# A two-layer streaming encoder: each feed-forward in two phases, and both parts of x in one 512 wide matmul

## The chip, the core and the metric

The kernel runs on one core of a Trainium2 chip. A time is the device time of one execution in microseconds (us), and less is better. TensorE multiplies a 128x128 block of weights that it holds with a stream of columns and adds the result into one of eight PSUM banks of 512 float32 columns. VectorE and ScalarE read PSUM and the on-chip memory and write back to the latter; GpSimd adds squares here. Every engine runs its own queue of instructions in order and waits for the others by semaphores.

## The reference

Two layers work on 256 tokens of width 1024. Each layer is, with all norms, gates and mixers cut to their names:

```
h = h + 0.5 * swiglu(rmsnorm(h, ffn1_norm), ffn1_w_up, ffn1_w_down)
h = h + token_mixer(rmsnorm(h, mix_norm), ...) @ w_out      # attention, retention, SSD, HGRN2
h = h + 0.5 * swiglu(rmsnorm(h, ffn2_norm), ffn2_w_up, ffn2_w_down)
gate = sigmoid(rmsnorm(h, ple_norm) @ ple_w_gate)
h = h + gate * (p[i] @ ple_w_proj)

def swiglu(h, w_up, w_down):
    gate, up = split(h @ w_up, 2)                           # 1024 -> 2 x 2816
    return (silu(gate) * up) @ w_down                       # 2816 -> 1024
```

A final rmsnorm ends it. All data are float32. The four feed-forwards (two in each layer) hold most of the arithmetic.

## The kernel before

The state `H` lies transposed: features on the 128 partitions, in eight tiles (`KD`) of 256 tokens (`S`) each. A product in nearly float32 precision is made of rounded operands: every weight and every x is split into a high part of the type float32r and the low rest, and three matmuls add high x high, high weight x low x, and low weight x high x. Line 247 in `prod` issues these three, each 256 columns wide.

Weights come as tiles of 128x1024 in the order of their use. `fetch` (line 155) loads one from memory on SyncE's queue into one of four `raw` buffers, ScalarE casts it to `wh` (line 164), VectorE subtracts to get `wl` (line 165), each with eight buffers. `weight` keeps two tiles fetched ahead in the program's order; a scheduler then orders each engine's queue, so that casts move forward until buffers are wanting.

A norm's scale is applied late: `Norm.part` (line 187) only multiplies by the norm's weight and splits (ScalarE line 192, VectorE line 193), `square` (line 200) squares on ScalarE and adds up on GpSimd, `scale` and `spread` sum the squares with small matmuls (line 108) and make a row `rb` of 1/rms for all tokens. It multiplies the results of the up matmuls, not x.

`ffn` (line 296) goes through 11 blocks `j` of 256 hidden columns. For each it makes gate and up (32 triples of matmuls into one bank of the kind `p` and one of the kind `m`), and then the part of the down product for the block before (16 triples into four banks of the kind `a`, which collect all 1024 output features over all j). Beside that VectorE and ScalarE make the product silu(gate) x up, 512 wide, and split it (lines 317 to 320 and `split`). After the last block `advance` (line 896) takes the four pairs of output tiles one after the other: `ffn_finish` scales and adds to `H`, `part` prepares the next x. The next stage's first group of matmuls runs over k in the outer loop, so that it can begin with the first pair.

After the second feed-forward of a layer the input p is loaded on ScalarE's queue (line 1016) and split. In layer 1 it is multiplied by `ple_w_proj` into four banks before the gate; in layer 2 `ending` does the same with tokens on the partitions, 512 columns wide (lines 924 to 926, gate in lines 937 to 939).

Of the kernel before, what the change touches and what calls it, by code (L numbers as in the profile page):

```python
# [9 lines left out]
F32 = mybir.dt.float32  # L10
# [9 lines left out]
P = 128  # L20
# [44 lines left out]
def trunk(ctx, tc, x, pt, par_d, con_d, w_d, ws_d, fin_d, out):  # L65
# [10 lines left out]
    cnt = [0]  # L76
    NB = {"h2": 4, "hp2": 1, "s2": 2, "m2": 7, "yh": 8, "yl": 8, "raw": 4, "wh": 8, "wl": 8}
    PB = {"p": 2, "m": 2, "a": 4}

    def T(shape, kind, dt=F32, bufs=2):  # L80
        cnt[0] += 1
        return wk.tile(shape, dt, name=f"{kind}_{cnt[0]}", tag=kind, bufs=bufs)

    def tw(kind, dt=F32, width=1024):
        if kind in ("raw", "wh", "wl"):
            return T([P, WIDE], kind, dt, NB[kind])[:, 0:width]
        return T([P, 512], kind, dt, NB[kind])

    def bank(which):
# [4 lines left out]
    def v2(t):  # L94
        return t.rearrange("p (a b) -> p a b", a=2)
# [33 lines left out]
    for t in kts + qts:  # L129
        G.memset(t, 0.0)  # L130
    xbp = cp.tile([P, 4, S + 3], F32, name="xbp")
    G.memset(xbp[:, :, 0:3], 0.0)
    identb = cp.tile([P, P], BF16, name="identb")
# [49 lines left out]
    class Norm:  # L183
        def __init__(self):
            self.h, self.l, self.sq = [], [], []

        def part(self, c, l, name, first=False):
            xh, xl = v2(tw("yh", F32R)), v2(tw("yl", F32R))
            for i in range(2):
                d = 2 * c + i  # L190
                w = prm(l, name, d)
                A.mul(xh[:, i], H[:, d], w)  # L192
                V.scalar_tensor_tensor(xl[:, i], H[:, d], w, xh[:, i].bitcast(F32),  # L193
                                       ALU.mult, ALU.subtract)
                self.h.append(xh[:, i])
                self.l.append(xl[:, i])
            if not first:
                self.square(c)

# [22 lines left out]
        def spread(self):  # L222
            for t in range(2):
                rows(self.b[:, 256 + t * P:256 + (t + 1) * P], self.col[:, t:t + 1])
            rb = cp.tile([P, S], F32, name=f"rb{cnt[0]}", tag="rb")
            A.copy(rb, self.b[:, 256:512])
            self.rb = rb.unsqueeze(1).broadcast_to([P, 2, S])

# [20 lines left out]

    def col_tiles(targets, xn, k_outer=False, arrival=None, lag=0):  # L250
        def one(b, w, m, k, terms=(0, 1, 2)):
            wh, wl = w[m]
            prod(b[:, m * S:(m + 1) * S], wh[:, k], wl[:, k], xn.h[k], xn.l[k],
                 k == 0 and m == 0, k == KD - 1, terms)
        if k_outer:
            units = [(b, w, m) for b, w in targets for m in range(2)]
            rank = arrival or (lambda u, k: k // 2)
            order = sorted((rank(u, k), u, k) for u in range(len(units)) for k in range(KD))
            for n in range(len(order) + lag):
                if n == len(order) * SCALE_AT // 32:  # L260
                    xn.scale()
                if n < len(order):
                    one(*units[order[n][1]], order[n][2], (0, 1))
                if n >= lag:
                    one(*units[order[n - lag][1]], order[n - lag][2], (2,))
            xn.spread()
        else:
            for b, w in targets:
                for m in range(2):
                    for k in range(KD):  # L270
                        one(b, w, m, k)

# [17 lines left out]
    def split(src):  # L290
        yh, yl = tw("yh", F32R), tw("yl", F32R)
        A.copy(yh, src)
        V.tensor_sub(yl, src, yh.bitcast(F32))
        return v2(yh), v2(yl)

    def ffn(xn, after_first=None, arrival=None, lag=0):
        acc = None
        prev = None
        for j in range(NJ):
            wg = by_column()  # L300
            wu = by_column()
            bg, bu = bank("p"), bank("m")
            col_tiles(((bg, wg), (bu, wu)), xn, k_outer=(j == 0), arrival=arrival, lag=lag)
            if j == 3 and after_first is not None:
                after_first()
            if prev is not None:
                if acc is None:
                    acc = [bank("a") for _ in range(4)]
                w, gh, gl = prev
                held = []  # L310
                for f in range(2):
                    if j == NJ - 1 and f == 1:
                        held.append((w[f], gh[:, f], gl[:, f]))
                    else:
                        down(acc, [(w[f], gh[:, f], gl[:, f])], j == 1 and f == 0, False)
            s, g = tw("m2"), tw("m2")
            V.tensor_mul(v2(s), v2(bg), xn.rb)
            A.activation(s, s, AF.Silu)
            V.tensor_mul(g, s, bu)
            gh, gl = split(g)  # L320
            prev = (by_row(), gh, gl)
        w, gh, gl = prev
        held += [(w[f], gh[:, f], gl[:, f]) for f in range(2)]
        down(acc, held, False, True)
        return acc

    def down(acc, terms, first, last):
        for m in range(8):
            for n, ((wh, wl), yh, yl) in enumerate(terms):
                cs = slice(m * P, (m + 1) * P)  # L330
                prod(acc[m // 2][:, (m % 2) * S:(m % 2 + 1) * S], wh[:, 0, cs], wl[:, 0, cs],
                     yh, yl, first and n == 0 and m % 2 == 0, last and n == len(terms) - 1)

    def ffn_finish(acc, rb, c):
        t = tw("m2")
        V.tensor_mul(v2(t), v2(acc[c]), rb)  # L336
        hp = flat(H[:, 2 * c:2 * c + 2])
        V.scalar_tensor_tensor(hp, t, 0.5, hp, ALU.mult, ALU.add)  # L338

# [27 lines left out]
    def mixer(l, xn):  # L367
# [16 lines left out]
        def column(w, b, m):  # L384
            wh, wl = w[m]
            for k in range(KD):
                prod(b[:, m * S:(m + 1) * S], wh[:, k], wl[:, k], xn.h[k], xn.l[k],
                     k == 0 and m == 0, k == KD - 1)

        def projections():  # L390
# [300 lines left out]
    def ssd(l, got, need):  # L691
        yield from need("xs", "bc", "small")
        _, dt, g = got["small"]
        xbc = tw("wl").rearrange("p (m t) -> p m t", m=4)
        for n, m in enumerate((2, 3, 0, 1)):
# [201 lines left out]
    def advance(update, l, name, first=False):  # L897
        xn = Norm()
        for c in range(4):
            update(c)  # L900
            xn.part(c, l, name, first)
        return xn
# [3 lines left out]

    def ending(acc, xn, l, ph, pl):

# [8 lines left out]
        for t in range(2):  # L917
# [10 lines left out]
            emb.append(o)  # L928
        xg = advance(lambda c: ffn_finish(acc, xn.rb, c), l, "ple")
        w = by_row(8)  # L930
# [62 lines left out]
    for st in steps:  # L993
        n = int(st[1])
        if st[0] == "x":
            nc.sync.dma_start(H[:, 2 * n:2 * n + 2], x[:, 2 * n:2 * n + 2])
            xn.part(n, 0, "ffn1", True)
        else:
            begin[n](int(st[2]))
# [7 lines left out]

    for l in range(DEPTH):
        acc = ffn(xn, *((load_constants, arrival, LAG) if l == 0 else (bounds,)))
        xn = advance(lambda c: ffn_finish(acc, xn.rb, c), l, "mix")  # L1010
        acc = mixer(l, xn)
        xn = advance(lambda c: V.tensor_add(hpair(c), hpair(c), acc[c]), l, "ffn2")  # L1012
        acc = ffn(xn)

        p_sb = tw("m2")
        A.dma_start(v2(p_sb), pt[l])
        ph, pl = split(p_sb)
        if l == DEPTH - 1:
            ending(acc, xn, l, ph, pl)
# [12 lines left out]
        xn = advance(lambda c: ffn_finish(acc, xn.rb, c), l, "ple")  # L1032
# [127 lines left out]
```

## Time and profile before

| | us |
|---|---|
| median of 3 runs (lowest, highest) | 1126.75 (1125.4, 1127.15) |
| the profiled execution | 1125.76 |
| its span, from the first instruction to the last | 1124.0 |
| TensorE busy | 1094.7 (97%) |
| VectorE busy | 749.3 (67%) |
| ScalarE busy | 568.6 (51%) |
| weights and inputs read | 190.66 MB |

A busy TensorE says only that matmuls are in flight: they overlap, so the time that one costs is the distance from its start to the next start, not its own duration. The distance can be had from two rows of the timeline and the count between them, or from the count of a window.

### The profile page before, as it was taken

How to read it: one execution, taken by the hardware profiler on the slowest of the kernel's cores; microseconds unless marked ns; L12 is line 12 of the kernel's file. 1: busy time of each engine (PE TensorE's matmuls, PEld its weight loads, DVE VectorE, ACT ScalarE, POOL GpSimd, SP SyncE). 2: the span in 40 equal slices, each digit the busy share in tenths (PEclk: the TensorE clock that was granted, in tenths of full speed). 3: DMA queues.
4: the chain of work that ended last, by engine and by line, in shares of the span. 5: the costliest groups of instructions: out<-in, count | busy, mean ns of one | idle time of the engine just before them, and what ended most of it. 6: DMA issues, size and time to landing. Idle time of an engine off the chain costs nothing.

```text
span 1124.0 us, 22113 instructions
## 1 busy us (share of the span) xinstructions
PE 1094.7 (97%) x9290; PEld 1069.4 (95%) x9290; DVE 749.3 (67%) x1082; ACT 568.6 (51%) x764; POOL 40.2 (4%) x39
## 2 busy tenths in 40 slices
PE   7999999999999999999999999998999999999996
PEld 7999999889899999999999999997899899999995
DVE  7655556799778555556975555577997765555584
ACT  7544444645576444444665444446446754444463
POOL 2000000200001000000100000011000100000011
PEclk9999999999999999999999999999999999999998
DMA  8866666135456666665656666642454476666631
GB/s 274 284 219 182 182 184 187 58 116 183 120 174 210 191 184 184 184 186 159 206 175 184 187 187 188 183 155 58 137 165 151 149 244 187 182 184 183 187 122 38
DMA packets 55445, 194.21 MB, mean 173 GB/s; under 512 B 6576, under 2 KB 7088, under 8 KB 55344
## 3 DMA queue, kind: packets, MB, share of 16 engines
q1 hardware_dynamic: 54192, 191.06, 55.5%
q10 hardware_dynamic: 1152, 1.72, 0.5%
q8 instruction: 73, 1.20, 0.4%
q14 instruction: 28, 0.23, 0.1%
HBM read 190.66 MB, written 1.05 MB: 171 GB/s over the span
## 4 chain that ended last, share of the span: by engine, by line
PE 81%; DVE 12%; ACT 3%; issue 2%; DMA 1%; ACTq 0%; DVEq 0%; SPq 0%
PE bank_p L247 30%; PE bank_m L247 23%; PE bank_a L247 22%; DVE wl L165 3%; DVE yl L193 2%; DMA raw<-w 1%; ACT wh L164 1%; DVE wl L628 1%; DVE qt L604 1%; DVE H L338 1%; PE bank_a L108 1%; DVE m L336 1%; ACT yh L192 0%; PE bank_m L883 0%; DVE H L1012 0%
## 5 line engine op out<-in xcount | busy, mean ns | idle before, releaser
L165 DVE TENSOR_TENSOR wl<-raw,wh 128x1024 fp32r<-128x1024 f32 (+2 forms) x360 | 435.8, 1218 | 255.6 <-ACT wh L164 255.2
L164 ACT CAST wh<-raw 128x1024 fp32r<-128x1024 f32 (+2 forms) x360 | 370.6, 1038 | 421.1 <-PE bank_p L247 138.5
L247 PE MATMUL bank_p<-yh,wh 128*128 128x256 f32 x1064 | 305.0, 287 | 6.2 <-ACT wh L164 6.2
L247 PE MATMUL bank_p<-yh,wl 128*128 128x256 f32 x1064 | 301.7, 284 | 0.9 <-DVE wl L165 0.9
L247 PE MATMUL bank_p<-yl,wh 128*128 128x256 f32 x1064 | 301.9, 284 | 0.0
L247 PE MATMUL bank_a<-yl,wh 128*128 128x256 f32 x896 | 252.9, 283 | 0.3 <-DVE yl L193 0.3
L247 PE MATMUL bank_a<-yh,wl 128*128 128x256 f32 x896 | 252.5, 282 | 0.0
L247 PE MATMUL bank_a<-yh,wh 128*128 128x256 f32 x896 | 252.0, 282 | 0.0
L247 PEld LDWEIGHTS bank_p<-yh,wh 128*128 128x128 f32 x1064 | 202.6, 190 | 8.1 <-ACT wh L164 6.2
L247 PE MATMUL bank_m<-yh,wl 128*128 128x256 f32 x712 | 201.3, 284 | 4.4 <-DVE wl L165 4.4
L247 PEld LDWEIGHTS bank_p<-yl,wh 128*128 128x128 f32 x1064 | 202.4, 190 | 1.2 <-DVE yl L193 0.2
L247 PEld LDWEIGHTS bank_p<-yh,wl 128*128 128x128 f32 x1064 | 201.9, 190 | 1.6 <-DVE wl L165 1.0
L247 PE MATMUL bank_m<-yh,wh 128*128 128x256 f32 x712 | 202.3, 284 | 0.0
L247 PE MATMUL bank_m<-yl,wh 128*128 128x256 f32 x712 | 202.0, 284 | 0.0
L247 PEld LDWEIGHTS bank_a<-yl,wh 128*128 128x128 f32 x896 | 169.5, 189 | 0.8 <-DVE yl L193 0.5
L247 PEld LDWEIGHTS bank_a<-yh,wl 128*128 128x128 f32 x896 | 169.5, 189 | 0.0
L247 PEld LDWEIGHTS bank_a<-yh,wh 128*128 128x128 f32 x896 | 169.2, 189 | 0.0
L247 PEld LDWEIGHTS bank_m<-yh,wl 128*128 128x128 f32 x712 | 135.7, 191 | 4.8 <-DVE wl L165 4.8
L247 PEld LDWEIGHTS bank_m<-yh,wh 128*128 128x128 f32 x712 | 136.7, 192 | 0.0
L247 PEld LDWEIGHTS bank_m<-yl,wh 128*128 128x128 f32 x712 | 136.4, 192 | 0.0
L204 POOL TENSOR_TENSOR m<-m,m 128x512 f32<-128x512 f32 x16 | 23.3, 1459 | 1018.1 <-ACT m L202 585.9
L193 DVE SCALAR_TENSOR_TENSOR yl<-H,par,yh 128x256 fp32r<-128x256 f32 x64 | 43.9, 715 | 11.9 <-ACT yh L192 11.9
(314 smaller groups left out, 866.5 us busy)
## 6 DMA issues: line engine op xcount, KB each, us to landing
raw<-w SPq DMA_DIRECT2D x348, 512.0 KB, 3.7
raw<-ws SPq DMA_DIRECT2D x4, 528.0 KB, 3.7
raw<-w SPq DMA_DIRECT2D x8, 256.0 KB, 4.7
con<-con SPq DMA_DIRECT2D x3, 512.0 KB, 6.4
H<-x SPq DMA_DIRECT2D x4, 256.0 KB, 5.1
m<-rk SPq DMA_DIRECT2D x8, 64.0 KB, 4.2
m<-rq SPq DMA_DIRECT2D x8, 64.0 KB, 2.0
m<-pt ACTq DMA_DIRECT2D x2, 256.0 KB, 3.2
```

The lines of the kernel that those rows point to most:

```text
L108: mm(o[r], lhsT[:, r], rhs, start=start, stop=stop, skip_group_check=True)
L164: A.copy(h[:, cs], r[:, cs])
L165: last_dve[0] = V.tensor_sub(lo[:, cs], r[:, cs], h[:, cs].bitcast(F32)).ins
L193: V.scalar_tensor_tensor(xl[:, i], H[:, d], w, xh[:, i].bitcast(F32), ALU.mult, ALU.subtract)
L204: G.tensor_add(sq, sq, self.sq.pop())
L247: mm(o, wl if n == 2 else wh, xl if n == 1 else xh, start=first and n == 0, stop=last and n == 2, skip_group_check=True)
L336: V.tensor_mul(v2(t), v2(acc[c]), rb)
L338: V.scalar_tensor_tensor(hp, t, 0.5, hp, ALU.mult, ALU.add)
L604: V.tensor_mul(o, q0, e0)
L628: V.copy_predicated(pf[r].rearrange("p (h c n two e) -> p c h n two e", h=8, c=2, two=2, e=L)[:, u, :, :, 1], K("lvl", m, m + 32)[r].rearr ...
```

## The change

Each feed-forward runs in two phases. In the first, all 22 tiles of 128 hidden columns are made, gate and up each in a bank of its own, in seven banks in turn; the products stay on the chip, high and low part side by side in 512 columns, in 22 places that the mixer uses at other times. In the second, one output tile at a time is made: 22 triples into one bank, then scaled, added to `H` and prepared as the next x at once. x and the products have their high and low part side by side, so that `prod2` needs one matmul of 512 columns with the high weight (both parts of x) and one of 256 with the low weight; the two halves of the bank are added afterwards by a copy on ScalarE and an addition on VectorE. The weights of the two phases are stored in the order of their use. The load of p comes after the whole feed-forward in the program, `xbp` is taken for each mixer, and the matmuls outside the feed-forwards keep the three of `prod`. `advance` goes on for the other stages.

```diff
+    def prod2(b, wh, wl, x, first, last, terms=(0, 1)):
+
+        if 0 in terms:
+            mm(b, wh, x, start=first, stop=False, skip_group_check=True)
+        if 1 in terms:
+            mm(b[:, S:], wl, x[:, 0:S], start=False, stop=last, skip_group_check=True)
+
...
+        def next_bank():
+            tags[0] += 1
+            return bank("pmpmaaa"[(tags[0] - 1) % 7])
...
+        def product(bg, bu):
+            t = tw("m2")
+            s, u = t[:, 0:S], t[:, S:]
+            A.copy(s, bg[:, S:])
+            V.tensor_add(s, s, bg[:, 0:S])
+            V.tensor_mul(s, s, xn.row)
+            A.activation(s, s, AF.Silu)
+            A.copy(u, bu[:, S:])
+            V.tensor_add(u, u, bu[:, 0:S])
+            V.tensor_mul(s, s, u)
+            g = next(homes)
+            A.copy(g[:, 0:S], s)
+            V.tensor_sub(g[:, S:], s, g[:, 0:S].bitcast(F32))
+            gs.append(g)
+
+        units = [unit() for _ in range(4)]
+        col_group(units, xn, one, ((0,), (1,)), arrival, lag)
+        for f in range(2):
+            product(units[2 * f][0], units[2 * f + 1][0])
+        for f in range(2, NF // P):
+            units = [unit(), unit()]
+            for u in units:
+                for k in range(KD):
+                    one(u, k)
+            if f == 7 and after_first is not None:
                 after_first()
...
+            product(units[0][0], units[1][0])
+
+        new = Norm()
+        n = 0
+        for m in range(KD):
+            b = bank("a")
+            for f in range(NF // P):
+                if n % KD == 0:
+                    wh, wl = (t.rearrange("p (a b) -> p a b", b=P) for t in weight(1)[0])
+                prod2(b, wh[:, n % KD], wl[:, n % KD], gs[f], f == 0, f == NF // P - 1)
+                n += 1
+            t = tw("m2")[:, 0:S]
+            A.copy(t, b[:, S:])
+            V.tensor_add(t, t, b[:, 0:S])
+            V.tensor_mul(t, t, xn.row)
+            V.scalar_tensor_tensor(H[:, m], t, 0.5, H[:, m], ALU.mult, ALU.add)
+            new.part(m, l, name)
+        return new
```

On TensorE, in the first feed-forward of layer 1, two blocks of k of one gate tile (before, then changed; `wh` and `wl` are the weight's two parts, `yh`, `yl` and `y2` those of x):

```order
L247 MATMUL bank_p87_540<-yh_13_97,wh_70_505 128x256
L247 MATMUL bank_p87_540<-yl_14_98,wh_70_505 128x256
L247 MATMUL bank_p87_540<-yh_13_97,wl_71_506 128x256
L247 MATMUL bank_p87_540<-yh_13_97,wh_70_505 128x256
L247 MATMUL bank_p87_540<-yl_14_98,wh_70_505 128x256
L247 MATMUL bank_p87_540<-yh_13_97,wl_71_506 128x256
```

```order
L257 MATMUL bank_p99_634<-y2_13_95,wh_91_573 128x512
L259 MATMUL bank_p99_634<-y2_13_95,wl_92_574 128x256
L257 MATMUL bank_p99_634<-y2_13_95,wh_91_573 128x512
L259 MATMUL bank_p99_634<-y2_13_95,wl_92_574 128x256
L257 MATMUL bank_p99_634<-y2_14_107,wh_91_573 128x512
```

Three instructions for a block of k became two, over the same 768 columns.

On ScalarE, in the middle of the first feed-forward (before, then changed; `m2` holds gate and product, `hp2` is one of the 22 places):

```order
L164 CAST wh_121_899<-raw_120_898 128x1024
L318 ACTIVATE m2_113_883<-m2_113_883 128x512
L164 CAST wh_124_905<-raw_123_904 128x1024
L164 CAST wh_127_911<-raw_126_910 128x1024
L292 CAST yh_115_888<-m2_114_884 128x512
```

```order
L360 COPY m2_147_908<-bank_a143_869 128x256
L166 CAST wh_181_1092<-raw_180_1091 128x1024
L364 CAST hp2_148_916<-m2_147_908 128x256
L356 COPY m2_157_965<-bank_a149_919 128x256
L166 CAST wh_185_1099<-raw_184_1098 128x1024
L359 ACTIVATE m2_157_965<-m2_157_965 128x256
L360 COPY m2_157_965<-bank_a153_926 128x256
L166 CAST wh_191_1149<-raw_190_1148 128x1024
```

Between the weight casts there now stand four instructions for each 128 hidden columns, two of which read PSUM.

On ScalarE at the end of layer 1's second feed-forward (before, then changed; `pt` is p, `H_64` the state):

```order
L292 CAST yh_821_6076<-m2_820_6072 128x512
L1016 DMA m2_829_6164<-pt 128x512
L164 CAST wh_859_6282<-raw_858_6281 128x1024
L292 CAST yh_830_6166<-m2_829_6164 128x512
L192 ACTIVATE yh_843_6237<-H_64,par0_65 128x256 x2
```

```order
L391 COPY m2_881_5518<-bank_a874_5461 128x256
L194 ACTIVATE y2_873_5458<-H_64,par0_65 128x256
L205 ACTIVATE m2_882_5525<-H_64 128x512
L1079 DMA m2_883_5527<-pt 128x512
L166 CAST wh_920_5773<-raw_919_5772 128x1024
L166 CAST wh_923_5779<-raw_922_5778 128x1024
L307 CAST y2_884_5529<-m2_883_5527 128x2x256
```

The load of p moved behind the last output tile's copy, scaling and square, and two weight casts stand between it and the cast of p.

## Rows read from the trace of the kernel before

**Rows 1.** The profile's page: engine share; bandwidth in 40 equal slices.
```profile
PE 1094.7 (97%) x9290; PEld 1069.4 (95%) x9290; DVE 749.3 (67%) x1082; ACT 568.6 (51%) x764; POOL 40.2 (4%) x39
...
GB/s 274 284 219 182 182 184 187 58 116 183 120 174 210 191 184 184 184 186 159 206 175 184 187 187 188 183 155 58 137 165 151 149 244 187 182 184 183 187 122 38
```

**Rows 2.** The chain of waits, by line.
```profile
PE bank_p L247 30%; PE bank_m L247 23%; PE bank_a L247 22%; DVE wl L165 3%; DVE yl L193 2%; DMA raw<-w 1%; ACT wh L164 1%; DVE wl L628 1%; DVE qt L604 1%; DVE H L338 1%; PE bank_a L108 1%; DVE m L336 1%; ACT yh L192 0%; PE bank_m L883 0%; DVE H L1012 0%
```

**Rows 3.** Windows: length, busy us (count) of PE, PEld, DVE, ACT, POOL; clock; DMA.
```profile
40.00:200.00 160.00, 160.00 (x1346) 160.00 (x1345) 90.80 (x92) 70.26 (x80) 1.29 (x1) 1.00 0.64 196
...
920.00:1080.00 160.00, 160.00 (x1350) 160.00 (x1349) 88.92 (x87) 68.31 (x76) 0.00 (x0) 1.00 0.62 187
```

**Rows 4.** Who waited for whom: us in total, times, longest us.
```profile
DVE wl L165 <- ACT wh L164: 255.2, 250, 2.0
...
ACT wh L164 <- PE bank_p L247: 138.5, 75, 4.2
ACT wh L164 <- PE bank_a L247: 116.9, 78, 2.1
...
PE bank_m L247 <- DVE wl L165: 4.4, 2, 2.3
```

**Rows 5.** Timeline of TensorE, start and duration in us; one window.
```profile
1084.16 0.39 PE L924 MATMUL bank_p<-wh,yh 128*128 128x512 f32 x1
...
1097.69 0.39 PE L939 MATMUL bank_a<-wh,yl 128*128 128x512 f32 x1
...
1103.32 0.48 PE L937 MATMUL bank_a<-wh,yh 128*128 128x512 f32 x1
...
1108.72 0.39 PE L939 MATMUL bank_a<-wh,yl 128*128 128x512 f32 x1
...
1084.30:1097.85 13.55, 13.55 (x61) 1.00 0.12 41
```

**Rows 6.** VectorE by form: count | busy us, mean ns of one | idle before.
```profile
L165 DVE TENSOR_TENSOR wl<-raw,wh 128x1024 fp32r<-128x1024 f32 x348 | 424.2, 1226 | 252.9 <-ACT wh L164 252.5
L193 DVE SCALAR_TENSOR_TENSOR yl<-H,par,yh 128x256 fp32r<-128x256 f32 x64 | 43.9, 715 | 11.9 <-ACT yh L192 11.9
...
L585 DVE TENSOR_TENSOR h<-lk,hb 128x256 f32<-128x256 f32 x12 | 5.0, 414 | 0.1
...
L728 DVE TENSOR_TENSOR s<-cbias,bank_m 128x256 f32<-128x256 f32 x4 | 1.6, 411 | 0.0
```

**Rows 7.** ScalarE by form.
```profile
L164 ACT CAST wh<-raw 128x1024 fp32r<-128x1024 f32 x348 | 361.7, 1047 | 418.5 <-PE bank_p L247 138.5 <-PE bank_a L247 114.4 <-PE bank_m L247 71.1
...
L192 ACT ACTIVATE yh<-H,par 128x256 fp32r<-128x256 f32 x64 | 29.0, 500 | 33.6 <-DVE H L338 27.2 <-DVE H L1042 2.5 <-DMA par<-par 2.2
...
L202 ACT ACTIVATE m<-H 128x512 f32<-128x512 f32 x32 | 19.8, 617 | 0.0
L591 ACT ACTIVATE kt<-h 128x256 f32<-128x256 f32 x14 | 5.5, 413 | 3.7 <-DVE h L585 3.2 <-DVE h L580 0.5
...
L226 ACT COPY rb<-bank_a 128x256 f32<-128x256 f32 x7 | 2.5, 363 | 0.4 <-PE bank_a L102 0.4
```

**Rows 8.** TensorE by form: the sums of squares.
```profile
L108 PE MATMUL bank_a<-ones,m 128*64 128x1 f32 x192 | 7.4, 199 | 1.8 <-ACT m L202 1.8
```

**Rows 9.** Timeline of TensorE before the first mixer, idle before in brackets.
```profile
209.16 0.63 PE L108 MATMUL bank_a<-ones,m 128*64 128x1 f32 x16 [0.82 <-ACT m L202]
```

**Rows 10.** DMA issues: count, KB each, median us to landing.
```profile
m<-pt ACTq DMA_DIRECT2D x2, 256.0 KB, 3.2
```

**Rows 11.** After the first mixer: timeline of TensorE and VectorE; the window behind.
```profile
342.63 0.39 PE L247 MATMUL bank_m<-yh,wl 128*128 128x256 f32 x1 [2.11 <-DVE wl L165]
...
338.39 2.51 DVE L193 SCALAR_TENSOR_TENSOR yl<-H,par,yh 128x256 fp32r<-128x256 f32 x2
...
342.60:346.00 3.40, 3.37 (x18) 3.37 (x19) 3.40 (x5) 0.69 (x1) 0.00 (x0) 0.62 0.62 167
```

More of the change, by code (lines that the diff above doesn't have):

```diff
@@ L184, in __init__, with part @@
         def __init__(self):
[L185 to L198, printed above, removed]
+            self.x, self.h, self.l, self.sq = [], [], [], []
+        def part(self, d, l, name, first=False):
+            if d % 2 == 0:
+                self.y = pair()
+            y = self.y[:, d % 2]
+            w = prm(l, name, d)
+            A.mul(y[:, 0], H[:, d], w)
+            V.scalar_tensor_tensor(y[:, 1], H[:, d], w, y[:, 0].bitcast(F32),
+                                   ALU.mult, ALU.subtract)
+            self.x.append(flat(y))
+            self.h.append(y[:, 0])
+            self.l.append(y[:, 1])
+            if d % 2 and not first:
+                self.square(d // 2)
         def square(self, c):
@@ L226, in spread @@
             A.copy(rb, self.b[:, 256:512])
+            self.row = rb
             self.rb = rb.unsqueeze(1).broadcast_to([P, 2, S])
@@ L254, in one @@
                  k == 0 and m == 0, k == KD - 1, terms)
+        units = [(b, w, m) for b, w in targets for m in range(2)]
         if k_outer:
[L256 to L266, printed above, removed]
-        else:
[L268 to L271, printed above, removed]
+            col_group(units, xn, one, ((0, 1), (2,)))
+        else:
+            for u in units:
+                for k in range(KD):
+                    one(u, k)
     def token_tiles(outs, w, xn, k0, first, last):
@@ L290, in split @@
     def split(src):
[L291 to L304, printed above, removed]
-                after_first()
[L306 to L338, printed above, removed]
+        y = pair()
@@ new lines, in split, with store, c @@
+        A.copy(y[:, :, 0], v2(src))
+        V.tensor_sub(y[:, :, 1], v2(src), y[:, :, 0].bitcast(F32))
+        return y[:, :, 0], y[:, :, 1]
+    def store():
+        def c(tag, **kw):
+            cnt[0] += 1
+            return cp.tile([P, 512], F32R, name=f"g_{tag}{cnt[0]}", tag=tag, **kw)
+        for tag in ("hq", "hv", "kk", "lk", "hb"):
+            yield c(tag)
+        for _ in range(NB["h2"]):
+            yield tw("h2", F32R)
+        for _ in range(3):
+            yield c("qk", bufs=3)
+        yield tw("hp2", F32R)
+        for tag in ("g0", "g1"):
+            yield c(tag)
+        for tag in ("sz", "hg", "rg"):
+            yield c(tag)
+        cnt[0] += 1
+        t = cp.tile([P, 4, S + 3], F32R, name=f"g_xbp{cnt[0]}", tag="xbp")
+        t = t.rearrange("p a b -> p (a b)")
+        yield t[:, 0:512]
+        yield t[:, 512:1024]
+        for _ in range(NB["s2"]):
+            yield tw("s2", F32R)
@@ new lines, in ffn, with one, unit @@
+    def ffn(xn, l, name, after_first=None, arrival=None, lag=0):
+        homes = store()
+        tags = [0]
+        gs = []
+        def next_bank():
+            tags[0] += 1
+            return bank("pmpmaaa"[(tags[0] - 1) % 7])
+        def one(unit, k, terms=(0, 1)):
+            b, (wh, wl) = unit
+            prod2(b, wh[:, k], wl[:, k], xn.x[k], k == 0, k == KD - 1, terms)
+        def unit():
+            return next_bank(), tuple(t.rearrange("p (a b) -> p a b", b=P)
+                                      for t in weight(1)[0])
+        def product(bg, bu):
[18 more added lines that the diff above has]
+            units = [unit(), unit()]
+            for u in units:
+                for k in range(KD):
+                    one(u, k)
+            if f == 7 and after_first is not None:
+                after_first()
+            product(units[0][0], units[1][0])
[15 more added lines that the diff above has]
+        return new
@@ L388, in column @@
                      k == 0 and m == 0, k == KD - 1)
+        xbp = cp.tile([P, 4, S + 3], F32, name=f"xbp{l}", tag="xbp")
+        G.memset(xbp[:, :, 0:3], 0.0)
+        got["xbp"] = xbp
         def projections():
@@ L900, in advance @@
             update(c)
-            xn.part(c, l, name, first)
+            for d in (2 * c, 2 * c + 1):
+                xn.part(d, l, name, first)
         return xn
@@ L996, in trunk @@
             nc.sync.dma_start(H[:, 2 * n:2 * n + 2], x[:, 2 * n:2 * n + 2])
-            xn.part(n, 0, "ffn1", True)
+            for d in (2 * n, 2 * n + 1):
+                xn.part(d, 0, "ffn1", True)
         else:
@@ L1008, in trunk @@
     for l in range(DEPTH):
[L1009 to L1010 removed]
+        xn = ffn(xn, l, "mix", *((load_constants, arrival, LAG) if l == 0 else (bounds,)))
         acc = mixer(l, xn)
         xn = advance(lambda c: V.tensor_add(hpair(c), hpair(c), acc[c]), l, "ffn2")
[L1013 removed]
+        xn = ffn(xn, l, "ple")
         p_sb = tw("m2")
@@ L1098, in ffn_tiles @@
         def ffn_tiles(up, down):
-            for j in range(NJ):
-                c = slice(j * 256, (j + 1) * 256)
-                tiles.extend(_by_column(up[:, c]))
-                tiles.extend(_by_column(up[:, NF + j * 256:NF + (j + 1) * 256]))
-                tiles.extend(_by_row(down[c]))
+            for j in range(NF // P):
+                for o in (0, NF):
+                    tiles.extend(_by_column(up[:, o + j * P:o + (j + 1) * P]))
+            blocks = down.reshape(NF // P, P, KD, P).transpose(1, 2, 0, 3).reshape(P, -1)
+            tiles.extend(blocks[:, i:i + 1024] for i in range(0, NF * KD, 1024))
         ffn_tiles(a["ffn1_w_up"][l], a["ffn1_w_down"][l])
```

29 lines of the change are left out of this document (20 added, 9 removed).

## The prediction

> **What bounds the kernel now.** I read the engine shares first, then the chain of waits, then the same counts over stretches, then the durations of single groups. The reader is to see in the shares that TensorE has work in 97% of the span [rows 1], and in the chain that 81% of it is matmuls at line 247, with VectorE a distant second [rows 2]. Inside a feed-forward there is no other limit: between 40 and 200 us and between 920 and 1080 us TensorE is busy for the whole 160 us at the full granted clock, while VectorE fills 91 and 89 us and ScalarE 70 and 68 us of it [rows 3]. The waits say the same from the other side: ScalarE's casts wait for TensorE to free a buffer (138.5 and 116.9 us), and VectorE waits for those casts (255.2 us) [rows 4]. Converted weights stand ready and TensorE sets the pace. So the time is a count of matmuls times their spacing, and the question is what the spacing becomes.
>
> **Spacing of the matmuls.** One 128x128 weight block meets x in three 256 wide matmuls now and in one 512 wide and one 256 wide afterwards: 768 columns either way, one instruction less. The two stretches of 160 us hold 1346 and 1350 matmuls, of which two or three hang over an edge: 160 us / 1344 = 119.0 ns and 160 / 1348 = 118.7 ns, so 118.9 ns each and 356.7 ns for three [rows 3]. The trace has 512 wide matmuls of the same number type at the end: 60 of them follow each other from 1084.16 to 1097.69 us, 59 spacings in 13.53 us, 229.3 ns each [rows 5] (the window on them counts 61, one of which is the 256 wide matmul before). A 512 wide one thus costs 8.5 ns less than two of 256. New triple: 229.3 + 118.9 = 348.2 ns.
>
> How many: one feed-forward has 22 blocks of columns x gate and up x 8 blocks of k = 352 triples, and 8 output tiles x 22 = 176 down, 528 in all; four feed-forwards make 2112. 2112 x 8.5 ns = 18.0 us saved. Bounds: a later run of 24 of the 512 wide matmuls goes from 1103.32 to 1108.72 us, 23 spacings of 234.8 ns [rows 5]; by it the saving is 3.0 ns x 2112 = 6.3 us. The 118.9 is known to 0.2 ns, which makes 8.9 ns and 18.8 us the other end. I take 229.3, since it is the longer run and the slow one holds a pause at its head.
>
> The page "TensorE: Matmul & The Clock Gate" of the Trainium skill (section "Wait — 56ns, not 53.3ns?") says that a warm matmul costs its columns at 2.4 GHz and about 2.5 ns fixed. By that the change would save 2.5 ns x 2112 = 5.3 us, an estimate. This trace does not agree on the size: 118.9 ns is 12.2 ns above 256 columns at 2.4 GHz, and 229.3 is 16.0 above 512.
>
> **What the change adds on VectorE and ScalarE.** In the first phase each product of 128 columns takes five VectorE instructions of 256 (two adds that read PSUM, two products, one subtraction) and four on ScalarE (two copies from PSUM, Silu, one cast). VectorE has such rows at 411 ns with a PSUM operand and 414 ns without, ScalarE at 363 ns for a copy from PSUM and 413 ns for a function [rows 6, 7]. With the two weight tiles of that product (1226 ns and 1047 ns each) VectorE has 2 x 1.226 + 5 x 0.414 = 4.52 us and ScalarE 2 x 1.047 + 2 x 0.363 + 2 x 0.413 = 3.65 us of work, while TensorE needs 16 x 0.3482 = 5.57 us. Both are hidden. The dearest 128x256 row on VectorE is 715 ns [rows 6], with which it would be 6.03 us and no longer hidden; that row belongs to places where GpSimd adds squares beside it, and the first phase has no GpSimd work, so I take 414. A copy queued on ScalarE waits for its gate or up block, and behind it stand casts for blocks four products later, so a late copy finds weights in stock. In the second phase an output tile takes 22 x 0.3482 = 7.66 us on TensorE, against 2.75 x 1.226 + 2 x 0.414 + 2 x 0.715 = 5.6 us on VectorE at most. Price of all this: nothing; without the cover, 6.03 - 5.57 = 0.46 us for each of 88 products.
>
> The weight stream is unchanged: half a megabyte for every eight triples, 188 GB/s at the new pace against the 187 to 196 GB/s moved now [rows 3], and the first slices of the span ran at 274 and 284 [rows 1].
>
> **The two handovers of a feed-forward.** Up to down: the first output tile reads all 22 products in order, so the last one is wanted 21 x 0.348 = 7.3 us after the first phase ends. On ScalarE its cast stands behind a weight cast whose buffer is freed after eight down triples (2.8 us); 2.8 + 1.05 + 0.41, then on VectorE one weight tile 1.23 and the subtraction 0.41, gives 5.9 us. It fits with 1.4 us over.
>
> Down to the next stage: today four pairs of H tiles are updated, scaled and squared after the end, and TensorE waits for the squares: 1.8 us in all [rows 8], of which 0.82 us before the first mixer [rows 9] and as much before the second. Afterwards seven of the eight tiles are done while TensorE still works; the last needs 0.363 + 0.414 + 0.414 + 0.715 + 0.500 + 0.617 = 3.0 us [rows 6, 7], and about 4.1 with the weight cast that stands ahead of it. Before the mixers TensorE first has 72 matmuls that do not need it (72 x 0.1189 = 8.6 us). I count 1.6 us saved. Before the gate in layer 1 only 36 matmuls (4.3 us) cover the same chain; I count nothing there, either way.
>
> **What is late next.** The load of p is now issued on ScalarE's queue after the last square, where before it stood among the casts before the end. After the end: 3.0 us for the tile, 3.2 us to landing [rows 10], 0.62 us for a 512 wide cast as for a 512 wide square [rows 7]: about 7 us and the handovers. TensorE has 60 matmuls (7.1 us) to do before it asks for p in layer 1, where two casts stand ahead of p's as well, and 30 of 512 columns (6.9 us) in layer 2. I take 0.5 us at each of the two places, with 0 and 2.0 as ends: +1.0 us, 0 to 4.
>
> **What stays.** After each mixer TensorE waits 2.2 us for a low weight part (4.4 us, two times) [rows 4], because two of VectorE's instructions take 2.51 us beside GpSimd; then the mean granted clock is 0.62 for 3.4 us, so for most of it the lower of its two levels, and only 18 matmuls pass, some 1.3 us late [rows 11]. The changed order has the same rows ahead of that weight part, and 3.25 us of work before it is needed against 3.1. I count no change; bounds -7 us (wait and lower clock go, twice) and +3.
>
> **The sum.** -18.0 - 1.6 + 1.0 = -18.6 us. The profiled execution took 1125.76 us (span 1124.0 and 1.76 around it), so 1107.2; the median of the runs is 1126.75, 1.0 above it, so I forecast 1108 us.
>
> **Rivals.**
> A (0.66), the forecast: 1108, own range 1104 to 1112.
> B (0.12): the 512 wide matmul saves only the 3.0 ns of the slow run. For it: that run lies among work on the other engines, and no row shows 512 and 256 in turn. Against: the long run. 1126.75 - 6.3 - 0.6 = 1120. The fixed 2.5 ns on the page "TensorE: Matmul & The Clock Gate" of the Trainium skill points to this case.
> C (0.05): the stalls after the mixers and the lower clock behind them also go: 1108 - 7 = 1101. Against: the same instructions stand ahead.
> D (0.05): p comes 2 us late twice and the clock falls behind each, as in rows 11: 1108 + 2 x (1.5 + 1.3) = 1114.
> E (0.06): VectorE becomes the bound. If its 256 wide instructions cost 715 ns, 88 products x 0.46 us = 40 us come onto the path and the kernel takes 1126.75 - 18.6 + 40 = 1148. The point from which it decides is (5.57 - 2.45) / 5 = 0.62 us an instruction. For it: VectorE goes from 57% to 81% in this phase, and five dependent steps pass between two engines. Against: 411 and 414 ns.
> F (0.06): no saving at all, a 512 wide one costing two of 256: 1126.
>
> **How the numbers follow.** No change means within 0.2%, 2.3 us, about what a measurement of this kernel can tell. Faster: A to D, 0.88; same: F, 0.06; slower: E, 0.06. The range 1102 to 1120 takes in A, B and D, and leaves out C, E and F with 0.17.
>
> **What would show it.** TensorE's matmul count falls by 2112 to about 7180; in a window inside the first phase the triple takes 348 ns; VectorE is at about 80% there and TensorE at 100%; no TensorE wait for squares before the mixers; a wait of up to 2 us for p's cast at the two ple stages. The forecast is wrong if TensorE shows repeated waits for casts, products or low parts within a feed-forward, or if the spacing after a 512 wide matmul is not near 229 ns.

## The result and the profile after

The changed kernel took 1110.82 us (median of 4 runs, 1109.53 to 1111.85), beside it the kernel before 1126.08 us (1124.87 to 1127.15): ratio 0.9864, 95% interval 0.9847 to 0.9881, 15.3 us less. The forecast was 1108 us. The profiled execution has a span of 1110.1 us against 1124.0. The time came out close to the forecast, but the experiments show that its largest term was put together wrongly: about 11 of the 15 us come with the two phases and three narrow matmuls as well, and in the second phase the wide one costs time against these.

The page of the changed kernel, engine shares; to be read beside [rows 1]:

```profile
PE 1080.3 (97%) x7178; PEld 960.0 (86%) x7178; DVE 839.0 (76%) x1454; ACT 638.8 (58%) x1063; POOL 39.9 (4%) x40
```

TensorE has exactly 2112 instructions fewer and is still the engine that is busy throughout. VectorE has 90 us more work and ScalarE 70 us; inside the feed-forwards TensorE waits for none of it, as its waits show (who waited for whom: us in total, times, longest us), to be read beside [rows 4]:

```profile
PE bank_p L257 <- DVE y L195: 7.8, 2, 6.6
PE bank_m L259 <- DVE wl L167: 5.0, 2, 2.7
PE bank_a L674 <- ACT wh L166: 2.1, 1, 2.1
...
PE bank_m L257 <- DVE m L1102: 0.2, 1, 0.2
```

The first row is the start (6.6 us until the first x, then one wait of 1.16 us), the second the two waits at the head of the feed-forwards behind the mixers, the third the second mixer. The last, 0.2 us, is for a bank that the gate of layer 1 (line 1102) frees for layer 2's first feed-forward. Behind the first group of a feed-forward there is no wait. So the pace counts. Windows of 60 us inside the first phase (60 to 120) and 40 us inside the second (150 to 190) of the first feed-forward; columns: length, then busy us and instructions of PE, PEld, DVE, ACT, POOL, then clock, DMA share, GB/s. First the kernel before, which has no phases:

```profile
60.00:120.00 60.00, 60.00 (x506) 60.00 (x505) 33.07 (x32) 25.68 (x29) 0.00 (x0) 1.00 0.64 186
150.00:190.00 40.00, 40.00 (x338) 40.00 (x337) 21.79 (x22) 17.31 (x19) 0.00 (x0) 1.00 0.61 185
```

The changed kernel:

```profile
60.00:120.00 60.00, 60.00 (x345) 52.61 (x344) 48.13 (x78) 37.33 (x68) 0.00 (x0) 1.00 0.67 211
150.00:190.00 40.00, 40.00 (x230) 34.90 (x229) 27.88 (x35) 20.50 (x29) 3.55 (x3) 1.00 0.59 187
```

With two matmuls over the edges taken off, 343 are 171.5 pairs in 60 us, 349.9 ns a pair, and 228 are 114 pairs in 40 us, 350.9 ns. From start to start over whole phases, the four feed-forwards have 349.7 to 350.9 ns in the first phase and 350.5 to 352.5 ns in the second (the 512 wide one 231.4 to 233.5, the 256 wide one 118.2 to 119.0). The forecast was 348.2. From 356.7 that makes 6.4 ns x 1408 = 9.0 us and 4.8 ns x 704 = 3.4 us: 12.4 us in place of 18.0.

### The profile page after: what moved, and what is told of

Its sections match the earlier page's. It is cut to its first block, busy times and chain, and to the rows that moved or that the text cites. A ratio compares the mean times of both kernels' runs of the same rounds, so it can differ in the third digit from the quotient of the medians.

```text
span 1110.1 us, 18572 instructions
## 1 busy us (share of the span) xinstructions
PE 1080.3 (97%) x7178; PEld 960.0 (86%) x7178; DVE 839.0 (76%) x1454; ACT 638.8 (58%) x1063; POOL 39.9 (4%) x40
## 4 chain that ended last, share of the span: by engine, by line
PE 84%; DVE 9%; ACT 3%; DMA 3%; issue 2%; SPq 0%; ACTq 0%; DVEq 0%
PE bank_a L257 27%; PE bank_a L259 14%; PE bank_p L251 10%; PE bank_m L257 8%; PE bank_p L257 8%; PE bank_m L259 4%; PE bank_p L259 4%; PE bank_a L251 3%; DVE wl L167 2%; DMA raw<-w 2%; DVE wl L690 1%; ACT wh L166 1%; DVE qt L666 1%; PE bank_a L112 1%; DVE y L195 1%
## 5 line engine op out<-in xcount | busy, mean ns | idle before, releaser
L257 PE MATMUL bank_a<-y,wh 128*128 128x512 f32 x576 | 203.0, 394 | 0.0
L259 PE MATMUL bank_a<-y,wl 128*128 128x256 f32 x576 | 161.8, 281 | 0.0
L257 PE MATMUL bank_p<-y,wh 128*128 128x512 f32 x416 | 150.6, 399 | 7.8 <-DVE y L195 7.8
L257 PE MATMUL bank_m<-y,wh 128*128 128x512 f32 x416 | 150.3, 397 | 0.2 <-DVE m L1102 0.2
L251 PE MATMUL bank_p<-y,wh 128*128 128x256 f32 x720 | 135.8, 287 | 0.0
L257 PEld LDWEIGHTS bank_a<-y,wh 128*128 128x128 f32 x576 | 108.1, 188 | 25.0
L259 PE MATMUL bank_m<-y,wl 128*128 128x256 f32 x416 | 116.1, 281 | 5.0 <-DVE wl L167 5.0
L259 PE MATMUL bank_p<-y,wl 128*128 128x256 f32 x416 | 117.1, 282 | 0.0
L251 PEld LDWEIGHTS bank_p<-y,wh 128*128 128x128 f32 x720 | 111.5, 189 | 2.7 <-issue 1.7
L251 PE MATMUL bank_p<-y,wl 128*128 128x256 f32 x360 | 102.3, 284 | 0.9 <-DVE wl L167 0.9
L257 PEld LDWEIGHTS bank_p<-y,wh 128*128 128x128 f32 x416 | 78.5, 189 | 26.7 <-ACT wh L166 6.6
L257 PEld LDWEIGHTS bank_m<-y,wh 128*128 128x128 f32 x416 | 78.6, 189 | 18.6 <-issue 0.5
L259 PEld LDWEIGHTS bank_p<-y,wl 128*128 128x128 f32 x416 | 78.6, 189 | 0.2
L251 PEld LDWEIGHTS bank_p<-y,wl 128*128 128x128 f32 x360 | 68.1, 189 | 1.5 <-DVE wl L167 1.0
L251 PEld LDWEIGHTS bank_a<-y,wh 128*128 128x128 f32 x384 | 59.6, 189 | 0.4 <-issue 0.3
L251 PE MATMUL bank_a<-y,wl 128*128 128x256 f32 x192 | 54.0, 284 | 0.0
```

The source lines that it names most:

```text
L251: mm(o, wl if n == 2 else wh, xl if n == 1 else xh, start=first and n == 0, stop=last and n == 2, skip_group_check=True)
L257: mm(b, wh, x, start=first, stop=False, skip_group_check=True)
L259: mm(b[:, S:], wl, x[:, 0:S], start=False, stop=last, skip_group_check=True)
```

## Experiments

All ratios are to the kernel before, run on the same chip; the median of before was 1125.5 to 1127.0 us in each set. Pairs of windows are the two from above.

**Three matmuls again, in two phases (e1_three).**

```diff
-            mm(b, wh, x, start=first, stop=False, skip_group_check=True)
+            mm(b[:, 0:S], wh, x[:, 0:S], start=first, stop=False, skip_group_check=True)
+            mm(b[:, S:], wh, x[:, S:], start=False, stop=False, skip_group_check=True)
```

> Two phases as in the changed kernel, but the 512 wide matmul is split again into two of 256 (all four feed-forwards). Theory (the pace of the matmuls makes the gain, the order of the work next to nothing): every triple is back at 356.7 ns, 2112 x 5.8 ns = 12.3 us above the changed kernel's 1110.8, so 1123 us (1121 to 1125), and about 2 to 3 us are left as the gain of the order (squares before the mixers). Rival (the two phases themselves make the gain: fewer handovers, whole tiles instead of blocks): it stays near 1111 to 1114 us.

Measured: 1114.49 us (1110.58 to 1118.11), ratio 0.9896 (0.9872 to 0.992). My theory fails here: without a single 512 wide matmul in the feed-forwards about 11 of the 15 us stay. The windows show where:

```profile
60.00:120.00 60.00, 60.00 (x506) 60.00 (x505) 46.70 (x77) 34.84 (x65) 0.00 (x0) 1.00 0.66 198
150.00:190.00 40.00, 40.00 (x355) 40.00 (x355) 28.07 (x35) 21.46 (x29) 3.55 (x3) 1.00 0.62 190
```

In the first phase 506 matmuls in 60 us are before's number to the last one: 504 / 3 = 168 triples, 357 ns. In the second phase 353 in 40 us are 113.3 ns each, 340 ns a triple: the same three instructions, 16.7 ns faster, at the same granted clock. Over 704 triples, some 40 of them still at the old pace, that is 664 x 16.7 = 11.1 us, which is the gain.

**Three matmuls in the second phase alone (e2_down_three).** `prod2` splits the 512 wide one, as above, only where the second phase calls it.

> As the changed kernel, but in the second phase (down) alone the 512 wide matmul is split into two of 256. Theory: the gain is so much per triple, wherever it stands; 704 triples x (356.7 - 352.0 = 4.7 ns) = 3.3 us above 1110.8, so 1114 us (1113 to 1115.5). Rival (the gain hangs on the first phase, or on the order): no change, 1111 us.

Measured: 1104.81 us (1103.22 to 1106.47), ratio 0.9815 (0.9793 to 0.9838). Both theories fail: taking the 512 wide matmul out of the second phase makes the kernel 6 us faster than the changed one.

```profile
60.00:120.00 60.00, 60.00 (x345) 52.55 (x345) 48.09 (x78) 37.28 (x68) 0.00 (x0) 1.00 0.65 212
150.00:190.00 40.00, 40.00 (x356) 40.00 (x355) 29.40 (x37) 20.86 (x29) 3.56 (x3) 1.00 0.59 195
```

The first phase has the changed kernel's pairs (345), the second e1's triples (356 against 355). So the 512 wide matmul is worth 6.4 ns a triple in the first phase and costs 351.9 - 340 = 11.9 ns in the second: -9.0 us and about +8 us, nearly nothing together. That agrees with e1_three against the changed kernel: 3.7 us apart in the medians, with intervals that overlap.

**High parts first, then low parts (e6_grouped).** Behind the first group, `one(u, k, (0,))` for the eight k of a tile, then `one(u, k, (1,))`, and the same in the second phase.

> As the changed kernel, but behind the first group of each feed-forward the eight 512 wide matmuls of a weight tile come first, then its eight 256 wide ones. Rival W (it is the turn from one width to the other that makes 350.9 ns of the forecast 348.2): 512 after 512 takes 229.3 ns and 256 after 256 118.9, 2.7 ns x 2000 = 5.4 us less, 1105.5 us. Theory F (a matmul of a width has its price whatever its neighbour): spacing in windows stays 350 to 351 ns a triple, 1110 to 1112 us.

Measured: 1109.7 us (1108.97 to 1110.4), ratio 0.9856 (0.9835 to 0.9877). The window in the first phase has 342 matmuls, but groups of eight do not fill it evenly with both widths. From start to start over whole phases a pair takes 349.9 to 350.3 ns in the first, as in the changed kernel. In the second it takes 346.3 to 348.0. The rows show it, the first matmul of the first and of the eighth output tile, with 7 x 22 = 154 pairs between them; first the changed kernel, 352.0 ns a pair:

```profile
134.84 0.40 PE L257 MATMUL bank_a<-g_hq,wh 128*128 128x512 f32 x1
...
189.05 0.40 PE L257 MATMUL bank_a<-g_hq,wh 128*128 128x512 f32 x1
```

Then e6_grouped, 347.9:

```profile
135.04 0.39 PE L257 MATMUL bank_a<-g_hq,wh 128*128 128x512 f32 x1
...
188.61 0.39 PE L257 MATMUL bank_a<-g_hq,wh 128*128 128x512 f32 x1
```

So the turn from one width to the other is not what makes 350 of 348 in the first phase, and theory F holds there. In the second, grouping takes some 4 ns off a pair, 3 us in all by the count; the medians differ by 1.1 us with intervals that overlap.

**A quarter of the weights' work (e7_quarter).** `units` keeps one of four tiles, used four times.

> Leaves out part of the work: in the feed-forwards (behind the first group) only one of four weight tiles is loaded, cast and split, and is used four times. The matmuls and the products stay as they are. Rival C (the load, casts and subtractions beside the matmuls slow them: contention): the triple falls from 350.9 ns to 348 or less, 1105 us or below. Theory F (the price of a matmul does not hang on its neighbours on other engines): 350 to 351 ns, 1109 to 1111 us.

Measured: 1112.64 us (1111.57 to 1116.71), ratio 0.9888 (0.9867 to 0.9908).

```profile
60.00:120.00 60.00, 60.00 (x343) 52.36 (x342) 27.64 (x60) 21.08 (x48) 0.00 (x0) 1.00 0.15 52
```

VectorE's work fell from 48 to 28 us, the transfers from 211 to 52 GB/s, and the pair stayed at 352 ns. So this load does not slow the pair. The time is not below the changed kernel's either: 1112.64 us lies above theory F's 1109 to 1111.

**All streamed numbers zero (e8_zero).**

```diff
+            if name in ("ffn1", "ffn2"):
+                w = 0.0
```

> As e2_down_three (512 + 256 in the first phase, three of 256 in the second), but the x of every feed-forward is multiplied by 0 instead of the norm's weight, so all numbers that stream through TensorE in both phases are zero; instructions, weights and order stay. What is to be told apart: in e2_down_three and e1_three a 256 wide matmul took 113.3 ns in the second phase and 118.9 in the first, with the same instructions, and the step came 0 to 8 us after the second phase began. Theory P (the pace hangs on the numbers that are multiplied): with zeros the first phase falls from 350 ns a triple to about 333 (a 512 wide one 220, a 256 wide one 113.3), 1408 triples x 17 ns = 24 us below e2_down_three's 1104.8, so 1081 us (1075 to 1090). Theory Q (it hangs on the place of the operands in memory or on the form of the program): first phase stays at 349 to 352, second at 340, 1104 us (1102 to 1107).

Measured: 1107.51 us (1106.98 to 1108.47), ratio 0.9847 (0.9831 to 0.9864). The time is half a microsecond above theory Q's range; the pace in both phases is that of e2_down_three (345 and 356):

```profile
60.00:120.00 60.00, 60.00 (x345) 52.60 (x344) 47.36 (x77) 36.31 (x68) 0.00 (x0) 1.00 0.63 205
150.00:190.00 40.00, 40.00 (x355) 40.00 (x355) 29.40 (x37) 20.66 (x29) 3.56 (x3) 1.00 0.60 197
```

The pace does not hang on the numbers that stream through; theory P falls.

**The products left out (e11_bare).**

```diff
             g = next(homes)
-            A.copy(g[:, 0:S], s)
-            V.tensor_sub(g[:, S:], s, g[:, 0:S].bitcast(F32))
+            A.copy(g[:, 0:S], bg[:, 0:S])
+            A.copy(g[:, S:], bu[:, 0:S])
```

(the nine lines above them, which make `s` and `u`, go as well).

> As e1_three, but the products of the first phase are left out: two copies on ScalarE take their place (half a bank each), VectorE has only the weights there. Theory S (the work beside the matmuls, VectorE's and ScalarE's reads of PSUM above all, makes 118.9 ns of 113.3): the first phase falls towards 340 ns a triple, 1408 triples x 16.6 = 23 us below 1114.5, so 1091 us, or part of it. Theory N (neighbours do not matter): 356 to 357 ns, 1112 to 1115 us.

Measured: 1114.07 us (1110.89 to 1115.55), ratio 0.9886 (0.9853 to 0.9918).

```profile
60.00:120.00 60.00, 60.00 (x506) 60.00 (x505) 25.75 (x21) 27.68 (x43) 0.00 (x0) 1.00 0.62 185
150.00:190.00 40.00, 40.00 (x356) 40.00 (x355) 28.16 (x35) 21.44 (x29) 3.56 (x3) 1.00 0.66 190
```

VectorE has 21 instructions in place of 77 in the first phase and TensorE the same 506. Theory S falls too.

**x read from the products' places (e10_place).**

```diff
-            g = next(homes)
+            g = places[8 + len(gs) % 14]
...
+        for k in range(KD):
+            V.tensor_copy(places[k], xn.x[k].bitcast(F32))
+            xn.x[k] = places[k]
```

> As e1_three (256 wide matmuls in both phases), but behind the first group of each feed-forward VectorE copies the eight x tiles into eight of the 22 places of the products, and the matmuls of the first phase read x there; the products then share the other 14 places, so later ones overwrite earlier ones and the output is not the reference's. Same instructions on TensorE, same banks and weights. What it tells apart: in e1_three a 256 wide matmul took 118.9 ns in the first phase (x in y2) and 113.3 in the second (x in the places). Theory L (it hangs on where the streamed operand lies): the first phase falls to 340 ns a triple, 4 x 320 triples x 16.6 ns = 21 us below e1_three's 1114.5, so 1093 us. Theory N (it does not): first phase stays at 356 to 357, 1114 to 1118 us with the copies.

Measured: 1117.48 us (1116.74 to 1118.13), ratio 0.9922 (0.9897 to 0.9946).

```profile
60.00:120.00 60.00, 60.00 (x515) 60.00 (x514) 48.39 (x80) 36.59 (x68) 0.00 (x0) 1.00 0.70 213
150.00:190.00 40.00, 40.00 (x345) 40.00 (x344) 28.39 (x36) 20.08 (x27) 3.56 (x3) 1.00 0.66 197
```

The time lies in theory N's range, but the pace follows neither theory: the first phase went from 357 to 351 ns a triple (513 / 3 = 171 in 60 us), and the second from 340 to 350 (343 / 3 in 40 us), though TensorE's instructions were the same but for the tiles that they name. What they name, or the waits that come with it, does move the pace, but not as "place of the products: fast". The banks and their order stayed, so these alone do not make the 340 of the second phase.

**x elsewhere on the chip (e12_layout).**

```diff
+    yk = pool("yk", 1)
...
-        return T([P, 2, 2, S], "y2", F32R, NB["y2"])
+        cnt[0] += 1
+        return yk.tile([P, 2, 2, S], F32R, name=f"y2_{cnt[0]}", tag="y2", bufs=NB["y2"])
```

> As e1_three, with every engine's instructions in the same order; only the tiles of x (y2) lie elsewhere on the chip: before the buffers of the weights instead of behind them, which moves the weights up by 32 KB a partition. The places of the products and the banks stay. What it tells apart: in e1_three a triple takes 356.7 ns in the first phase and 340 in the second with the same instructions. Theory L (the spacing hangs on where the operands lie towards each other): a triple of the first or of the second phase differs from e1_three's by 3 ns or more, and the time from its 1114.5 us by 4 us or more, in either direction (first phase at 340: 1091; second at 357: 1126). Theory N (the place does not matter; it is the form of the second phase that makes 340): 356 to 357 and 340, with the step in the same triples, 1112 to 1117 us.

Measured: 1112.98 us (1111.55 to 1115.1), ratio 0.989 (0.9871 to 0.9908): theory N by time and pace. The windows have 506 and 356. Even the place in the program where the pace steps up stayed. The timeline of e1_three, each row the first matmul of an output tile (the first two tiles of the first feed-forward, then the first three of the second):

```profile
136.55 0.29 PE L257 MATMUL bank_a<-g_hq,wh 128*128 128x256 f32 x1
144.05 0.28 PE L257 MATMUL bank_a<-g_hq,wh 128*128 128x256 f32 x1
...
463.90 0.28 PE L257 MATMUL bank_a<-g_hq,wh 128*128 128x256 f32 x1
471.68 0.28 PE L257 MATMUL bank_a<-g_hq,wh 128*128 128x256 f32 x1
479.18 0.28 PE L257 MATMUL bank_a<-g_hq,wh 128*128 128x256 f32 x1
```

The same rows of e12_layout:

```profile
136.03 0.29 PE L259 MATMUL bank_a<-g_hq,wh 128*128 128x256 f32 x1
143.53 0.28 PE L259 MATMUL bank_a<-g_hq,wh 128*128 128x256 f32 x1
...
463.65 0.28 PE L259 MATMUL bank_a<-g_hq,wh 128*128 128x256 f32 x1
471.43 0.28 PE L259 MATMUL bank_a<-g_hq,wh 128*128 128x256 f32 x1
478.93 0.28 PE L259 MATMUL bank_a<-g_hq,wh 128*128 128x256 f32 x1
```

22 triples take 7.50 us in the first feed-forward's first tile, 7.78 in the second's, then 7.50, in both kernels to the hundredth (and 7.49 and 7.78 in e11_bare). In e2_down_three and e8_zero, which share another order on TensorE, it is the other way round: 7.80 in the first feed-forward and 7.49 in the second. So the pace goes with TensorE's own stream of instructions. The starts in the trace of e1_three also differ in kind: in the window of the first phase they lie 112 to 128 ns apart, most of them 119 or 120, and in that of the second every one is 113 or 114 from the next. No kernel here shows that even run in a first phase, and e10_place shows it in neither. What in the stream sets it stays open. That it is the form of the second phase, as theory N has it, is not shown: e10_place has that form at 350 ns. By the sizes of the buffers in the source, the move in e12_layout was by multiples of 512 bytes (x by 20 x 4224 = 84,480, weights by 8 x 4096 = 32,768), so that a finer alignment of the operands was not tried.

**VectorE's cover (e4_plus2, e5_plus4).** Two, then four more instructions for each product:

```diff
+            for _ in range(4):
+                V.tensor_mul(u, s, xn.row)
```

> As the changed kernel with two more VectorE instructions of 128x256 for every product of the first phase (their results are overwritten). By my sum VectorE then has 4.52 + 2 x 0.414 = 5.35 us for each product and TensorE 16 x 0.350 = 5.60: still hidden, 1111 us (1110 to 1112.5). Rival (the cover is thinner than the sum, because VectorE waits for ScalarE's casts and copies in between): 1114 us or more, with TensorE waiting for low parts in the first phase.

> As the changed kernel with four more VectorE instructions of 128x256 for every product of the first phase (their results are overwritten). By my sum VectorE has 4.52 + 4 x 0.414 = 6.18 us for each product against TensorE's 5.60: 0.58 us x 80 products = 46 us slower, less some 5 us of stock at the beginning of each feed-forward (4 times), so 1140 to 1157 us. Rival (VectorE is not what a product waits for, or the instructions overlap): under 1120 us.

Measured: 1113.59 us (1111.06 to 1116.25), ratio 0.988 (0.9856 to 0.9903), and 1113.62 us (1112.19 to 1118.32), ratio 0.9893 (0.9868 to 0.9917). The first lies between its range and the rival's, and its interval reaches into both; its trace has no wait behind the first group of a feed-forward. The second misses by 26 us and more: my sum of durations was wrong, and the rival's time came. VectorE in e5_plus4, a window of the second feed-forward and four rows of the timeline:

```profile
360.00:450.00 90.00, 90.00 (x514) 78.59 (x513) 87.98 (x181) 54.52 (x98) 0.00 (x0) 1.00 0.57 194
```

```profile
402.01 0.42 DVE L364 TENSOR_TENSOR m<-m 128x256 f32<-128x256 f32 x1
402.34 0.42 DVE L360 TENSOR_TENSOR m<-m,rb 128x256 f32<-128x256 f32 x1
402.68 1.22 DVE L167 TENSOR_TENSOR wl<-raw,wh 128x1024 fp32r<-128x1024 f32 x1
403.81 0.42 DVE L367 TENSOR_TENSOR g_qk<-m,g_qk 128x256 fp32r<-128x256 f32 x1
```

Rows that follow each other overlap: one of 0.42 us is followed after 0.33 or 0.34, one of 1.22 after 1.13. A product then costs VectorE 2 x 1.13 + 9 x 0.335 = 5.28 us and not 6.18; TensorE needs 5.60. VectorE is 98% busy and just keeps up; TensorE waits once in each of two feed-forwards, 0.47 and 1.34 us, for a product.

**The low weight later after the mixers (e3_lag12, e9_both).** e9_both is e2_down_three with the same edit.

```diff
-        xn = ffn(xn, l, "ple")
+        xn = ffn(xn, l, "ple", lag=12)
```

> As the changed kernel, but in the feed-forwards behind the mixers the low weight's matmul runs 12 places behind the high weight's in the first group (before: at once). Theory (TensorE waits there for the low weight part alone, 2.91 and 2.41 us in the changed kernel): 12 x 0.233 = 2.8 us of other matmuls stand before the first one that needs it, both waits go, 1110.8 - 5.3 + 0.2 = 1105.7 us (1105 to 1108). Rival (the wait only moves: the next weight tiles and the next x parts are as late as the low part): 1109 to 1111 us, with new waits within 10 us of the same place.

> e2_down_three with the low weight's matmul 12 places behind in the first group after each mixer, as in e3_lag12. If the two edits add up: 1104.8 - 2.6 = 1102.2 us (1100.5 to 1104), with 340 ns a triple in the second phase and no wait of over 0.5 us for a low part after the mixers. If the wait that goes only lets another come: 1104 to 1106.

Measured: 1108.17 us (1105.29 to 1109.0), ratio 0.983 (0.9807 to 0.9852), and 1101.41 us (1099.07 to 1103.41), ratio 0.979 (0.9772 to 0.9809). After the first mixer, first in the changed kernel:

```profile
336.82 0.40 PE L257 MATMUL bank_m<-y,wh 128*128 128x512 f32 x1
339.96 0.39 PE L259 MATMUL bank_m<-y,wl 128*128 128x256 f32 x1 [2.75 <-DVE wl L167]
```

In e3_lag12:

```profile
339.15 0.40 PE L257 MATMUL bank_m<-y,wh 128*128 128x512 f32 x1
340.36 0.39 PE L259 MATMUL bank_m<-y,wl 128*128 128x256 f32 x1 [0.81 <-DVE wl L167]
```

In e9_both:

```profile
337.58 0.38 PE L262 MATMUL bank_m<-y,wl 128*128 128x256 f32 x1 [0.30 <-DVE wl L167]
...
346.28 0.43 PE L106 MATMUL bank_a<-con,ry 128*128 128x128 f32 x2 [1.36 <-DVE ry L246]
```

In e3_lag12 the waits shrink and do not go: from 2.75 to 0.81 us and, after the second mixer, from 2.25 to 0.83. That is 3.4 us, of which 2.6 show in the medians; the intervals of the ratios still touch, and 1108.17 lies just outside both ranges. In e9_both a wait of 1.36 us for the norm's row comes instead after the first mixer. Its 1101.41 us is what the two edits make if they add up, within their noise: the fastest kernel here, 9 us under the changed one.

## Why the prediction came out right, and which step of it failed

- **Spacing of the matmuls** (-18.0): measured -12.4 us. The term was mis-sized, and its ground failed. The 512 wide matmul takes 231.4 to 233.5 ns in the stream, not 229.3 as in [rows 5], so 6.4 and 4.8 ns are saved and not 8.5. And the sentence "a 512 wide one thus costs 8.5 ns less than two of 256" took 118.9 ns as the price of a 256 wide one anywhere. e1_three shows that in the second phase two of them cost 226.7 ns, and the 512 wide one there 231.8 to 233.5. No row of a feed-forward in the trace before could have shown it: gate and up (banks `p` and `m`) and down (bank `a`) had the same spacing there, 48 matmuls in 5.72 us and 96 in 11.43 us, 119 ns each:

```profile
67.60 0.28 PE L247 MATMUL bank_a<-yh,wh 128*128 128x256 f32 x1
...
73.32 0.28 PE L247 MATMUL bank_p<-yh,wh 128*128 128x256 f32 x1
...
84.75 0.28 PE L247 MATMUL bank_a<-yh,wh 128*128 128x256 f32 x1
```

  A rival "two phases alone make most of the gain" was missing.
- The page "TensorE: Matmul & The Clock Gate" of the Trainium skill (section "Wait — 56ns, not 53.3ns?") gives columns at 2.4 GHz and about 2.5 ns fixed. The runs do not agree: above the columns stand 6.6 ns (113.3), 12.2 ns (118.9) and 18.1 to 20.2 ns (231.4 to 233.5).
- **What bounds the kernel**: right, but the 81% of the chain is all of TensorE's; line 247 has 30 + 23 + 22 = 75% of it [rows 2].
- **VectorE and ScalarE hidden** (0): right, with more room than I worked out. Rival E's point, 0.62 us an instruction, was set too low because the durations overlap.
- **Squares before the mixers** (-1.6): right. The group that had 1.8 us of waits in [rows 8] now has none:

```profile
L112 PE MATMUL bank_a<-ones,m 128*64 128x1 f32 x192 | 7.1, 199 | 0.0
```

- **p late** (+1.0): nothing came. TensorE waits for p in neither layer, and the load lands in 3.4 us. The one wait near it, 0.2 us (L1102 above), comes behind the gate, for a bank. The other work of TensorE covers it.
- **After the mixers** (0, -7 to +3): 2.75 and 2.25 us instead of 2.11 and 2.3 [rows 4, 11], within the bounds. The lower clock behind them did not come in this execution, but behind the second mixer's wait of 2.1 us. Two windows of the changed kernel, behind the wait at 339.96 and behind the one that ends at 772.45:

```profile
340.00:344.00 4.00, 4.00 (x23) 3.55 (x24) 4.00 (x5) 1.34 (x2) 0.00 (x0) 1.00 0.62 181
...
772.00:776.00 4.00, 3.55 (x16) 3.30 (x16) 3.86 (x13) 1.68 (x4) 0.00 (x0) 0.57 0.13 22
```

- **The start**, which I did not count: the first matmul now wants both parts of x (6.62 against 6.18 us), and TensorE waits 1.16 us for the third pair's low part. The row that spreads the first norm stands at 24.68 us against 22.37: +2.3 us.

Together: -12.4 - 1.6 + 2.3 = -11.7 us; the last matmul starts 14.2 us earlier (1100.33 against 1114.52). Of the 2.5 us that are missing, half of 3.4 us = 1.7 us would be the one stretch at the lower clock fewer before the end (one against two); the rest I did not separate. Against the sum of -18.6 the profiled executions are 4.4 us short: 5.6 too much for the spacing and 2.3 not counted, less 1.0 for p and those 2.5. That the time came out within 3 us is in part luck: errors on one side met others on the other.

## What to carry to other kernels

Before a wider instruction is credited with a gain, run the same order with the narrow ones: here that alone kept about 11 of 15 us, and the wide one in the first phase with narrow ones in the second was some 6 us faster than the wide one in both and some 10 us faster than narrow ones in both. A spacing read in one program is not the price of the instruction: three of 256 took 357 ns everywhere in the feed-forwards before, and 340 in the second phase of the same work. Whether an engine keeps up is worked out from starts to starts of queued rows, not from their durations.

## What the runs showed of the hardware that I had not expected

- The same three 256 wide matmuls take 340 ns or 356 to 357 ns a triple at full granted clock. The step comes at the same triple in kernels with the same order on TensorE, and is not moved by the numbers (e8_zero), by the work of VectorE and ScalarE on the products (e11_bare) or by a coarse move of the operands (e12_layout). e10_place, where the matmuls name other tiles, does not have it. Its cause is open.
- A VectorE instruction on 128x256 that shows 0.42 us is followed after 0.335 us; one of 128x1024 that shows 1.22 us after 1.13 us.
- TensorE's granted clock fell to the lower of its levels behind a wait of 2.14 us and stayed at the upper behind one of 2.75 us in the same execution.
